# Where large tiles start in SBUF: from 128 bytes past a multiple of 256 to multiples of 256, with two families 160 and 96 bytes past one

## The chip, the cores and the metric

The kernel runs on one core of a Trainium2 chip. The metric is the device time of one launch in microseconds (us). Before the change the median of two runs is 1065.82 us (1065.74 and 1065.90). The host only lays arrays out ahead of the launch.

## What is computed

Two decoder layers and a last RMSNorm, all in float32, for one sequence of 512 positions and a model width of 1024. Cut to what matters:

```
for layer in range(2):
    h = rms_norm(x, norm_g)                              # 512 x 1024
    proj = h @ w_in                                      # 8704 columns, cut into 13 parts
    a = diff_attention(aq, ak, av) * silu(az)            # 4 heads
    c = short_conv(cx, cb, cc, conv_w) * silu(cz)
    r = retention(rq, rk, rv) * silu(rz)                 # 4 heads
    g = sigmoid(gates)                                   # 3 x 1024 columns of proj
    merged = sum(g[i] * ((a, c, r)[i] @ w_branch[i]) for i in range(3))
    x = x + merged @ w_out
out = rms_norm(x, final_norm_g)
```

## The kernel before

Activations lie transposed: channels on the 128 partitions, the 512 positions along the row, so that one tile of 128 x 512 float32 takes 2048 bytes of each partition. Every float32 product is made of three matmuls in `float32r` (`mm3`, lines 190 to 193): an operand is split into a high part, which is rounded, and a low part, which is the rest (`split`, line 186: ScalarE copies the high part, VectorE or GpSimd subtracts), and the three products hi x hi, hi x lo and lo x hi are added up in one PSUM bank. The first operand of `T.matmul` after the output is the stationary one, which LDWEIGHTS loads; the second is the moving one.

Weights come in chunks of 128 x 1024, in the order of `chunk_order`, by one DMA each into `wraw`, and are split into `whi` and `wlo` (4096 bytes of each partition, three buffers each). `proj` (line 422) makes 128 output columns from one chunk: 24 matmuls, whose stationary operands are 128 x 128 slices of `whi` and `wlo` and whose moving operands are the eight pairs of `h` tiles (tag "h", 16 buffers). `merge` (line 621) adds the product of a branch's four pairs of `xb` tiles with a chunk of `w_branch`; its last round leaves the merged rows `m` as eight pairs of tiles with the tag "vm". `out_proj` (line 676) has these `vm` tiles as moving operand and slices of `w_out` as stationary one; in the last layer it works on halves of 256 columns. Before `out_proj` the same 16 buffers hold the values of attention and retention: there `vm` is the stationary operand and the tiles with the tag "st" are the moving one (lines 527 and 611). In `values` (line 367) `xb` is stationary and `whi`/`wlo` are moving.

TensorE's instructions stand in an order that the code gives (`tick` and `at` put the attention and retention steps between the projections); the other engines' order is that of the program, with semaphores where operands ask for them.

All tiles come from three SBUF pools, each a row of tags in the order in which they are first asked for: `small` (the tags in `SMALL`), `sb` (nearly everything) and `odd` (only `wu`, whose rows are 2056 bytes). `t` (line 168) picks the pool by the tag, `tr` (line 172) asks for a `float32r` tile. Because every tag in `sb` takes a multiple of 256 bytes, all tiles of `sb` start at the same place within 256 bytes, and where that is follows from the size of `small`: 128 bytes past a multiple of 256.

Of the kernel before, what the change touches and what calls it, by code (L numbers as in the profile page):

```python
# [10 lines left out]
F32 = mybir.dt.float32  # L11
# [7 lines left out]
P = 128  # L19
# [135 lines left out]
def tile_hybrid_trunk(ctx: ExitStack, tc: tile.TileContext, xT, w, prm, lam, tab, cmat, outT):  # L155
    nc = tc.nc

    def pool(name, bufs=1, **kw):
        return ctx.enter_context(tc.tile_pool(name=name, bufs=bufs, **kw))

    SMALL = ("par", "eps", "lam_e", "ones_p", "ones_d", "nlam0", "nlam1", "gsub0", "gsub1", "rtok", "nm", "sm")
    small, sb, odd = pool("small"), pool("sb"), pool("odd")
    ps = pool("ps", space=PSUM)
# [2 lines left out]
    def t(tag, bufs, shape=(P, S), dt=F32):  # L168
        home = small if tag in SMALL else odd if tag == "wu" else sb
        return home.tile(list(shape), dt, tag=tag, bufs=bufs, name=tag)  # L170

    def tr(tag, bufs, shape=(P, S)):
        return t(tag, bufs, shape, F32R)

    def pj():
        return ps.tile([P, S], F32, tag="pj", bufs=NPJ, name="pj")
# [30 lines left out]
    def split_next():  # L207
        if not raws:
            prefetch()
        if raws:  # L210
            raw = raws.pop(0)
            hi, lo = tr("whi", 3, (P, 1024)), tr("wlo", 3, (P, 1024))
            for c in range(0, 1024, 512):
                c = slice(c, c + 512)
                if pos[0] or parts or c.start:
                    split(hi[:, c], lo[:, c], raw[:, c], G if c.start else V)
                else:
                    V.tensor_copy(hi[:, c], raw[:, c])
                    lo_part(lo[:, c], raw[:, c], hi[:, c])
            parts.append((hi, lo))  # L220
# [53 lines left out]
    nc.sync.dma_start(cm, cmat)  # L274
    ident, negmask, tri = (cm[:, i * P:(i + 1) * P] for i in range(3))
    ones_p = tr("ones_p", 1, (P, P))
    A.copy(ones_p, cm[:, 3 * P:4 * P])
    ones_d = t("ones_d", 1, (P, 1))
# [23 lines left out]

    H = [slice(0, 64), slice(64, 128)]
    klo = [tr("klo", 4) for _ in range(4)]
    for n, lo in enumerate(klo):
        G.memset(lo[H[1 - n % 2]].bitcast(F32), 0.0)
# [44 lines left out]
    for l in range(DEPTH):  # L351
# [59 lines left out]
        h = []  # L411
# [338 lines left out]
```

## Time and profile before

| | |
|---|---|
| median of the runs | 1065.82 us |
| profiled execution, its own time | 1065.34 us |
| its span, first to last instruction | 1063.5 us |
| PE, matmuls | 1053.9 us, 99% of the span, 5010 instructions |
| PEld, weight loads | 881.7 us, 83% |
| DVE (VectorE) | 681.9 us, 64% |
| ACT (ScalarE) | 503.0 us, 47% |
| POOL (GpSimd) | 318.7 us, 30% |
| granted TensorE clock | 0.998 of full speed, the 2.4 GHz level |

Matmuls overlap in the profile: a record runs from the matmul's start to its last result, and the next one starts before that. How fast TensorE goes is therefore read from the distance between two starts, here called the gap; the record is longer than the gap by a constant part in steady running.

### The profile page before, as it was taken

The numbers are of one execution on the slowest core, as the hardware profiler recorded it, in microseconds if no ns is written. First come the engines' busy times: TensorE is split into PE (matmuls) and PEld (weight loads), VectorE is DVE, ScalarE is ACT, GpSimd is POOL, SyncE is SP. The second block draws the span as 40 slices with busy tenths as digits, with TensorE's granted clock in tenths as the row PEclk, the third lists the DMA queues.
The fourth block names the chain that finished last, engine by engine and source line by source line (L and its number), as shares of the span: only waits on it lengthen the run. The fifth ranks groups of instructions, "written<-read, shape, count | busy, mean of one in ns | idle before, by whom it ended". The sixth has DMA issues, their size and how long they took to land.

```text
span 1063.5 us, 13847 instructions
## 1 busy us (share of the span) xinstructions
PE 1053.9 (99%) x5010; PEld 881.7 (83%) x5010; DVE 681.9 (64%) x1168; ACT 503.0 (47%) x943; POOL 318.7 (30%) x253
## 2 busy tenths in 40 slices
PE   9999999999999999999999999999999999999997
PEld 6888888888888888888888888888888888888896
DVE  8687686765677566345528876868556956654444
ACT  6454354543554554334434535445354645543353
POOL 6222232221233333232412212332123233333264
PEclk9999999999999999999999999999999999999999
DMA  6323222232234222444432232223213432133453
GB/s 258 106 93 100 88 71 96 83 119 85 74 119 139 77 85 78 128 129 149 149 99 83 87 109 80 80 84 119 96 60 100 139 100 80 61 107 129 128 190 119
DMA packets 34340, 113.64 MB, mean 107 GB/s; under 512 B 3936, under 2 KB 3936, under 8 KB 34272
## 3 DMA queue, kind: packets, MB, share of 16 engines
q1 hardware_dynamic: 34128, 112.50, 32.4%
q8 instruction: 39, 0.64, 0.3%
q14 instruction: 29, 0.24, 0.1%
q10 hardware_dynamic: 144, 0.26, 0.1%
HBM read 108.55 MB, written 4.19 MB: 106 GB/s over the span
## 4 chain that ended last, share of the span: by engine, by line
PE 93%; DVE 5%; ACT 1%; issue 1%; DMA 0%; SPq 0%; DVEq 0%; ACTq 0%
PE pj L191 28%; PE pj L192 28%; PE pj L193 28%; PE pa L466 3%; PE pa L192 1%; PE pa L193 1%; DVE wa L414 1%; PE pa L191 1%; DVE wlo L184 1%; PE pa L592 1%; DVE h L184 1%; DVE vm L382 1%; ACT h L187 1%; DVE xb L362 0%; PE pa L499 0%
## 5 line engine op out<-in xcount | busy, mean ns | idle before, releaser
L184 POOL TENSOR_TENSOR wlo<-wraw,whi 128x512 fp32r<-128x512 f32 x184 | 251.8, 1371 | 628.0 <-ACT whi L187 582.2
L191 PE MATMUL pj<-h,whi 128*128 128x512 f32 x960 | 379.4, 395 | 0.0
L192 PE MATMUL pj<-h,whi 128*128 128x512 f32 x960 | 374.7, 390 | 0.2
L193 PE MATMUL pj<-h,wlo 128*128 128x512 f32 x960 | 374.7, 390 | 0.0
L187 ACT CAST whi<-wraw 128x512 fp32r<-128x512 f32 x367 | 216.3, 617 | 220.9 <-PE pj L192 141.1
L184 DVE TENSOR_TENSOR wlo<-wraw,whi 128x512 fp32r<-128x512 f32 x184 | 153.1, 833 | 125.5 <-ACT whi L187 124.5
L193 PEld LDWEIGHTS pj<-h,wlo 128*128 128x128 f32 x960 | 180.2, 188 | 38.9 <-DVE wlo L184 0.3
L192 PEld LDWEIGHTS pj<-h,whi 128*128 128x128 f32 x960 | 180.5, 188 | 35.7 <-DVE h L184 1.1
L191 PEld LDWEIGHTS pj<-h,whi 128*128 128x128 f32 x960 | 180.4, 188 | 35.4
L191 PE MATMUL pj<-xb,whi 128*128 128x512 f32 x192 | 75.0, 391 | 0.0
L192 PE MATMUL pj<-xb,whi 128*128 128x512 f32 x192 | 74.9, 390 | 0.0
L193 PE MATMUL pj<-xb,wlo 128*128 128x512 f32 x192 | 74.7, 389 | 0.0
L579 ACT ACTIVATE p<-pa,nm 128x128 f32<-128x128 f32 (+3 forms) x64 | 33.5, 527 | 69.2 <-DVE nm L576 69.0
L503 DVE RECIPROCAL e<-e 128x512 f32<-128x512 f32 x16 | 53.6, 3351 | 18.0 <-ACT e L502 18.0
L187 ACT CAST st<-pa 128x256 fp32r<-128x256 f32 (+2 forms) x80 | 29.8, 373 | 70.5 <-DVE pa L521 40.5
L191 PE MATMUL pj<-vm,whi 128*128 128x256 f32 (+1 forms) x192 | 61.3, 319 | 0.0
L192 PE MATMUL pj<-vm,whi 128*128 128x256 f32 (+1 forms) x192 | 61.1, 318 | 0.0
L193 PE MATMUL pj<-vm,wlo 128*128 128x256 f32 (+1 forms) x192 | 61.1, 318 | 0.0
L636 DVE SCALAR_TENSOR_TENSOR wb<-wa,pj 128x512 f32<-128x512 f32 x32 | 22.0, 687 | 41.5 <-PE pj L193 38.3
L184 DVE TENSOR_TENSOR st<-pa,st 128x256 fp32r<-128x256 f32 (+2 forms) x80 | 33.6, 420 | 17.1 <-ACT st L187 16.5
L193 PEld LDWEIGHTS pj<-xb,wlo 128*128 128x128 f32 x192 | 36.0, 188 | 7.6
L191 PEld LDWEIGHTS pj<-xb,whi 128*128 128x128 f32 x192 | 36.1, 188 | 7.3
(132 smaller groups left out, 1433.6 us busy)
## 6 DMA issues: line engine op xcount, KB each, us to landing
wraw<-w SPq DMA_DIRECT2D x183, 512.0 KB, 3.4
tab<-tab SPq DMA_DIRECT2D x10, 512.0 KB, 3.4
xm<-xT SPq DMA_DIRECT2D x15, 256.0 KB, 3.7
xsave<-xm SPq DMA_DIRECT2D x8, 256.0 KB, 2.0
xm<-xsave SPq DMA_DIRECT2D x8, 256.0 KB, 2.6
outT<-p SPq DMA_DIRECT2D x8, 256.0 KB, 2.1
wraw<-w SPq DMA_DIRECT2D x2, 256.0 KB, 3.4
xm<-xT ACTq DMA_DIRECT2D x1, 256.0 KB, 3.0
```

The lines of the kernel that those rows point to most:

```text
L184: eng.tensor_tensor(lo, x, hi, op=ALU.subtract)
L187: A.copy(hi, x)
L191: T.matmul(out, wh, xh, start=start, stop=False)
L192: T.matmul(out, wh, xl, start=False, stop=False)
L193: T.matmul(out, wl, xh, start=False, stop=stop)
L382: V.scalar_tensor_tensor(lo, banks[tt], rtok[:, tt:tt + 1], hi, op0=ALU.mult, op1=ALU.subtract)
L414: V.scalar_tensor_tensor(hk, x[k], ng[k], rrow, op0=ALU.mult, op1=ALU.mult)
L466: T.matmul(o, ac[i][:, asl], bc[i][:, bsl], start=i == 0, stop=i == 1)
L503: V.reciprocal(r, r)
L579: A.activation(pc[:, :n], sp[:, :n], AF.Exp, bias=nm, scale=0.125, accum_out=sm)
L592: T.transpose(tp[:, j * P:(j + 1) * P], p1[:, j * P:(j + 1) * P], ident)
L636: V.scalar_tensor_tensor(y, g, 1.0, o, op0=ALU.add, op1=ALU.mult)
```

## The change

```
-
     SMALL = ("par", "eps", "lam_e", "ones_p", "ones_d", "nlam0", "nlam1", "gsub0", "gsub1", "rtok", "nm", "sm")
...
+
+    GAP, gaps = {"vm": 40, "h": 48, "st": 40}, {}
+
     def tr(tag, bufs, shape=(P, S)):
+        if tag in GAP and tag not in gaps:
+            gaps[tag] = t("gap_" + tag, 1, (P, GAP[tag]))
         return t(tag, bufs, shape, F32R)
+
+    small.tile([P, 32], F32, tag="fill", bufs=1, name="fill")
```

`fill` puts 128 bytes into `small`, so that the pools behind it start 128 bytes later. When `tr` is first asked for "vm", "h" or "st", a tile of 160, 192 or 160 bytes is put into `sb` ahead of that tag. No instruction reads or writes these tiles. On each of the five engines the changed program has the same instructions with the same waits in the same order; line numbers behind the change are larger by 6. What differs is where tiles start in each partition:

| tiles | bytes past a multiple of 256, before | after |
|---|---|---|
| `wraw`, `xm`, `wa`, `wb`, `xb`, `klo`, `qk`, `whi`, `wlo`, `e1`, `e2` | 128 | 0 |
| `vm` (values; later the merged rows m) | 128 | 160 |
| `h`, `tab`, `ez`, `p0`, `p1` | 128 | 96 |
| `st`, `wc`, `sq`, `wu` | 128 | 0 |
| `ones_p` (in `small`) | 160 | 32 |

## Rows read from the trace of the kernel before

**Rows 1.** The page: the span, engines' busy time (share) and instructions, the chain.
```profile
span 1063.5 us, 13847 instructions
...
PE 1053.9 (99%) x5010; PEld 881.7 (83%) x5010; DVE 681.9 (64%) x1168; ACT 503.0 (47%) x943; POOL 318.7 (30%) x253
...
PE 93%; DVE 5%; ACT 1%; issue 1%; DMA 0%; SPq 0%; DVEq 0%; ACTq 0%
```
**Rows 2.** Groups by form, PE: out<-in, tile, shape, xcount | busy us, mean ns | idle before.
```profile
L191 PE MATMUL pj<-h,whi 128*128 128x512 f32 x960 | 379.4, 395 | 0.0
L192 PE MATMUL pj<-h,whi 128*128 128x512 f32 x960 | 374.7, 390 | 0.2
L193 PE MATMUL pj<-h,wlo 128*128 128x512 f32 x960 | 374.7, 390 | 0.0
...
L191 PE MATMUL pj<-vm,whi 128*128 128x256 f32 x128 | 36.4, 284 | 0.0
...
L191 PE MATMUL pj<-vm,whi 128*128 128x512 f32 x64 | 24.9, 389 | 0.0
...
L193 PE MATMUL pa<-st,vm 128*128 128x256 f32 x40 | 11.3, 283 | 0.0
...
L193 PE MATMUL pa<-st,vm 128*128 128x128 f32 x24 | 6.6, 273 | 0.0
...
L193 PE MATMUL pa<-st,vm 128*128 128x512 f32 x8 | 3.2, 395 | 0.0
...
L193 PE MATMUL pa<-st,vm 128*128 128x384 f32 x8 | 2.7, 336 | 0.0
```
**Rows 3.** Timeline of PE, a steady stretch: start us, record us, engine line op.
```profile
51.93 0.39 PE L191 MATMUL pj<-h,whi 128*128 128x512 f32 x1
52.16 0.39 PE L192 MATMUL pj<-h,whi 128*128 128x512 f32 x1
...
56.69 0.39 PE L191 MATMUL pj<-h,whi 128*128 128x512 f32 x1
```
**Rows 4.** Timeline of PE, the last layer's out_proj.
```profile
1039.72 0.28 PE L193 MATMUL pj<-vm,wlo 128*128 128x256 f32 x1
...
1040.92 0.28 PE L191 MATMUL pj<-vm,whi 128*128 128x256 f32 x1
```
**Rows 5.** Timeline of all engines where a weight load came late.
```profile
22.62 0.39 PE L193 MATMUL pa<-whi,xb 128*128 128x512 f32 x1
22.62 0.19 PEld L191 LDWEIGHTS pj<-whi,xb 128*128 128x128 f32 x1
22.85 0.39 PE L191 MATMUL pj<-whi,xb 128*128 128x512 f32 x1
...
23.38 0.19 PEld L192 LDWEIGHTS pj<-wlo,xb 128*128 128x128 f32 x1 [0.56 <-DVE wlo L184]
23.38 0.50 PE L192 MATMUL pj<-wlo,xb 128*128 128x512 f32 x1
```
**Rows 6.** Timeline of PE around one pair of matmuls with `ones_p`.
```profile
138.18 0.40 PE L193 MATMUL pj<-h,wlo 128*128 128x512 f32 x1
138.42 0.39 PE L499 MATMUL pa<-st,ones_p 128*128 128x512 f32 x1
138.65 0.39 PE L500 MATMUL pa<-st,ones_p 128*128 128x512 f32 x1
...
141.18 0.39 PE L192 MATMUL pj<-h,whi 128*128 128x512 f32 x1
```
**Rows 7.** Timeline of PE behind four short matmuls.
```profile
122.08 0.27 PE L466 MATMUL pa<-klo,qk 128*128 128x128 f32 x1
122.19 0.45 PE L191 MATMUL pj<-h,whi 128*128 128x512 f32 x1
122.47 0.40 PE L192 MATMUL pj<-h,whi 128*128 128x512 f32 x1
```
**Rows 8.** Waits: engine, line, what ended them, us in total, times, longest.
```profile
POOL wlo L184 <- ACT whi L187: 582.2, 154, 8.9
ACT whi L187 <- PE pj L192: 141.1, 85, 5.6
DVE wlo L184 <- ACT whi L187: 124.5, 72, 4.7
```

## The prediction, made before the changed kernel was run

> **What bounds the kernel now.** I began with the page. PE is busy for 99% of the span and the chain of work that ended last runs through PE for 93% of it [rows 1], so only what TensorE does between one matmul's start and the next can move the time by much. The other engines have room: ACT, POOL and part of DVE's work wait for each other and for TensorE for hundreds of microseconds [rows 8].
>
> The groups by form say which matmuls these are. The three lines of `mm3` with `h` as moving operand and 512 columns come 960 times each, 2880 in all; with `vm` moving there are 3 x 64 = 192 of 512 columns and 3 x 128 = 384 of 256 columns; with `vm` stationary there are 3 x (40 + 24 + 8 + 8) = 240 [rows 2].
>
> Then the gap. In the timeline of a steady stretch 21 gaps take 56.69 - 51.93 = 4.76 us, 226.7 ns each [rows 3]. At 2.4 GHz, one column a cycle, 512 columns are 213.3 ns, so 13.3 ns are lost in each. With 256 columns, ten gaps take 1.20 us, 120.0 ns each [rows 4], against 106.7 ns: again 13.3 ns. This loss is what the change could touch. It is in 2880 + 192 + 384 = 3456 matmuls whose two operands move against each other, together 3456 x 13.3 = 46 us, and no more than this can be won in them.
>
> **What the change does, part by part.** It adds no instruction, no wait and no DMA; all engines' rows stand as before. Three things differ.
>
> *Everything 128 bytes further.* `whi`, `wlo`, `xb`, `qk`, `klo`, `st` go from 128 to 0 past a multiple of 256 together. Matmuls between these have both operands moved alike. Nothing in the trace has an operand at 0, so the trace gives no price for this; below, it is one of the ways to the fast rival. I take 0.
>
> *`h` at 96 and `vm` at 160 as moving operands, weights at 0.* Before, both operands of every one of these matmuls start at the same place within 256 bytes; after, they are 96 and 160 bytes apart, and the moving one no longer starts at a multiple of 64. The trace has one matmul whose operands are apart: `ones_p` as stationary operand lies at 160, its moving `st` at 128. Around such a pair the gaps are no longer steady: the load of `ones_p` runs under the matmul before it, whose gap reads 0.24 us and whose record grows from 0.39 to 0.40, and from 138.18 to 141.18 us 13 gaps take 3.00 us, 230.8 ns each, until the steady 0.39 is back [rows 6]. So TensorE does feel where operands start, by 230.8 - 226.7 = 4.1 ns a matmul while it is out of step, and it falls back into step by itself. The same happens behind short matmuls, which disturb the rhythm without any odd address: a record of 0.45 us, a gap of 0.28, then 0.40 [rows 7].
>
> Is the steady loss of 13.3 ns due to the load that runs under the matmul? Where a load came late, by 0.56 us, the matmul at 22.85 us ran without a load under it, and its record is 0.39 us like that of its neighbours [rows 5]. So the 13.3 ns look like the moving operand's own, not a quarrel with the weights. That says the relation of the two addresses has little to win in steady running, and that a new relation shifts the step in which both settle. What it may win is the time out of step: the records of `h` average 395, 390 and 390 ns where 389 is the steady value (the `vm` row with 512 columns), that is 960 x 6 + 960 x 1 + 960 x 1 = 7.7 us over the steady rate [rows 2]. Bounds for this part: -7.7 us if all of it went, +3456 x 4.1 = +14 us if TensorE never got into step. Part of the 7.7 us is the price of short matmuls as such and stays. I take half, -3.8 us.
>
> *`vm` at 160 as stationary operand, `st` at 0.* These 240 matmuls have the shape of the `ones_p` case, 32 bytes off. Between 0 and 240 x 4.1 = +1.0 us; I take +0.5, since two of three matmuls here have 256 or fewer columns and their records of 283 and 273 ns [rows 2] are long against their columns anyhow. The `ones_p` pair itself stays 32 bytes off, 16 pairs at 13 x 4.1 = 0.05 us, 0.9 us in all, unchanged.
>
> On VectorE, ScalarE and GpSimd the same operations read and write at new places. Their cover is their waiting: 582 us of POOL's and 124 us of DVE's idle time is for ACT's split, and 141 us of ACT's is for TensorE [rows 8]. If that cover failed in one place, the next weight load would be late, as in rows 5, at about half a microsecond each time. I take 0.
>
> Sum, against the profiled execution: 1065.3 - 3.8 + 0.5 = 1062.0 us. Its own time is 1065.34 us, span 1063.5 plus 1.8 around it; the median of the runs is 0.5 us above it, which I leave aside.
>
> **A rule against the change.** Rows 5 show a matmul that is no shorter without a load under it, and rows 6 a load that lengthens the matmul above it. The Trainium skill, page "TensorE: Matmul & The Clock Gate", section "Step-by-step: what each phase is for", says that TensorE reads the moving operand and the weights through two independent ports, so that loading weights takes nothing from the running matmul. By that rule where the two start against each other can't matter, and the sum would be the time before, 1065.3 us; rows 5 agree with it (0.39 us either way), rows 6 do not.
>
> **Rivals.**
>
> *Nothing moves.* The steady gap is the moving operand's own and the same at any of these places, and TensorE settles as often as before. For it: rows 5, and that the same 226.7 ns and 389 ns stand for `h`, `xb` and `vm`. Against it: rows 6. Time: 1065.3 us, or 1065.8 by the median. Chance 0.16.
>
> *Faster by over one step: the loss in the steady gap goes down.* The change sets the moving operands 96 and 160 bytes off the weights, on either side of half of 256. If the 13.3 ns (32 cycles) come from both reads starting at the same place within 256 bytes in the same hundredth of a microsecond (22.62 and 22.62 in rows 5), setting them apart takes half or all of it away. Half: 3456 x 6.7 = 23 us, 1042 us. All: 46 us, 1019 us. It passes 2% (21.3 us) when the gap of 512 columns falls to about 220.5 ns. For it: the loss is there in each matmul, and all matmuls of the trace but those with `ones_p` have both operands at the same place, so the trace has never shown another relation in steady running. Against it: rows 5, and that the only other relation made gaps longer. Chance 0.31, of which 0.28 passes 2%. The same page's section "Back-to-back issue gap" gives N/2.4 + 2.5 ns as the spacing, 215.8 ns for 512 columns; by it there would be an estimated 3456 x 10.9 = 38 us to win, 1028 us, while the trace shows 226.7.
>
> *Slower: TensorE no longer gets into step.* All 3456 matmuls get operands that are an odd multiple of 32 bytes apart, as those with `ones_p` are, and the disturbance that rows 6 show for a single pair becomes the rule. At the mean of that stretch, 4.1 ns, it is +14 us: 1079 us. At 6 ns it is +21 us, 1086 us, which is where it passes 2%; at the loss of one more 13.3 ns it would be +46 us, 1111 us. For it: the sign in rows 6. Against it: the stretch in rows 6 ends by itself within 13 matmuls. Chance 0.21, of which 0.17 passes 2%.
>
> **How the numbers follow.** The forecast, within 2% and slightly faster, has 0.32. Below 1027 us lies the part of the fast rival in which nearly all of the loss goes, about 0.08; above 1086 us the worse part of the slow one, about 0.12. So the range is 1027 to 1086 us; the likeliest case's own range is 1057.6 (all of the 7.7 us) to 1068. Over 2% (about what a measurement of this kernel can tell from no change) faster: 0.28. Within 2%: 0.32 + 0.16 + 0.03 + 0.04 = 0.55. Slower: 0.17.
>
> **What would show it.** Right: the steady gap with `h` in the timeline is still 226 to 227 ns, records 389 ns, and the means of 395, 390 and 390 ns fall by up to 6, 1 and 1. The fast rival: steady gaps at or below 220 ns, records of `h` at 383 ns or less, `vm` with 256 columns below 120. The slow one: means of `h` at 393 ns and above, gaps that change from matmul to matmul through whole projections. The part for `vm` as stationary operand is wrong if the 256-column row of 283 ns moves by more than 4. The forecast as a whole is wrong if the 13.3 ns depend on where the moving operand itself starts, which no row of before can show.

## The result and the profile after

The changed kernel takes 1084.01 us (1083.72 and 1084.30) against 1065.82 before: a ratio of 1.0171, with a 95% interval of 1.0154 to 1.0188. It is slower by 18.2 us. The forecast said 1062, slightly faster; the time lies in its range, on the side of the slow rival.

First the page of the changed kernel: span, busy times, the chain.

```profile
span 1082.5 us, 13847 instructions
...
PE 1071.8 (99%) x5010; PEld 881.2 (81%) x5010; DVE 681.2 (63%) x1168; ACT 502.9 (46%) x943; POOL 319.3 (29%) x253
...
PE 97%; DVE 1%; ACT 0%; DMA 0%; issue 0%; SPq 0%; DVEq 0%; ACTq 0%
```

The span has grown by 19.0 us and PE's busy time by 17.9, against [rows 1]. No other engine's busy time has moved by more than 0.7 us. So it is the matmuls themselves that take longer; the 1.1 us by which PE's idle time has grown is for the most part waiting for low parts of weights, in the last row below (0.3 us before, 1.6 now). Which matmuls, the groups by form of PE say (lines 197 to 199 are 191 to 193 of before):

```profile
L197 PE MATMUL pj<-h,whi 128*128 128x512 f32 x960 | 383.4, 399 | 0.0
L199 PE MATMUL pj<-h,wlo 128*128 128x512 f32 x960 | 380.2, 396 | 0.0
L198 PE MATMUL pj<-h,whi 128*128 128x512 f32 x960 | 379.6, 395 | 0.0
...
L198 PE MATMUL pj<-xb,whi 128*128 128x512 f32 x192 | 75.5, 393 | 0.0
...
L197 PE MATMUL pj<-vm,whi 128*128 128x256 f32 x128 | 36.1, 282 | 0.0
...
L197 PE MATMUL pj<-vm,whi 128*128 128x512 f32 x64 | 25.4, 396 | 0.0
...
L198 PE MATMUL pj<-wlo,xb 128*128 128x512 f32 x64 | 25.2, 393 | 1.6 <-DVE wlo L190 1.6
```

Two rows of before that [rows 2] does not show:

```profile
L191 PE MATMUL pj<-xb,whi 128*128 128x512 f32 x192 | 75.0, 391 | 0.0
L192 PE MATMUL pj<-xb,whi 128*128 128x512 f32 x192 | 74.9, 390 | 0.0
```

With `h` the mean records rise from 395, 390 and 390 ns [rows 2] to 399, 395 and 396. With `vm` and 512 columns they rise from 389 to 396. With `vm` and 256 columns they fall, from 284 to 282. And the matmuls of `xb`, whose two operands have both moved alike, rise too (390 to 393 on the line shown).

The timeline of PE at the same 21 matmuls as in [rows 3] shows what a steady stretch looks like now:

```profile
52.51 0.40 PE L197 MATMUL pj<-h,whi 128*128 128x512 f32 x1
52.75 0.40 PE L198 MATMUL pj<-h,whi 128*128 128x512 f32 x1
...
57.42 0.39 PE L197 MATMUL pj<-h,whi 128*128 128x512 f32 x1
```

21 gaps take 4.91 us, 233.8 ns each instead of 226.7, and records of 0.39 and 0.40 us alternate to the end of the stretch. TensorE never gets into the step of before.

Taking all starts of both traces in order and subtracting gap from gap, the 19.0 us are: 15.4 in the 2880 matmuls with `h` (5.4 ns each), 1.5 in the 192 of 512 columns with `vm` (7.6 ns each), 1.5 in the 576 with `xb` moving, 0.5 in the 384 with `xb` stationary, minus 0.5 in the 384 of 256 columns, and 0.6 in small groups. The 0.5 with `xb` stationary is not the change's: the same sum gives 0.5 there in the run below with all tiles at 160, in which no two of these operands are apart.

### The profile page after: what moved, and what is told of

It is laid out like the page before. It is cut to its first block, busy times and chain, and to the rows that moved or that the text cites. A ratio compares the mean times of both kernels' runs of the same rounds, so it can differ in the third digit from the quotient of the medians.

```text
span 1082.5 us, 13847 instructions
## 1 busy us (share of the span) xinstructions
PE 1071.8 (99%) x5010; PEld 881.2 (81%) x5010; DVE 681.2 (63%) x1168; ACT 502.9 (46%) x943; POOL 319.3 (29%) x253
## 4 chain that ended last, share of the span: by engine, by line
PE 97%; DVE 1%; ACT 0%; DMA 0%; issue 0%; SPq 0%; DVEq 0%; ACTq 0%
PE pj L197 29%; PE pj L198 29%; PE pj L199 29%; PE pa L472 3%; PE pa L199 2%; PE pa L198 2%; PE pa L197 2%; PE pa L598 1%; DMA xm<-xT 0%; DVE xb L368 0%; PE pa L506 0%; PE pa L505 0%; DVE p L714 0%; DVE e L333 0%; PE pa L341 0%
## 5 line engine op out<-in xcount | busy, mean ns | idle before, releaser
L197 PE MATMUL pj<-h,whi 128*128 128x512 f32 x960 | 383.4, 399 | 0.0
L199 PE MATMUL pj<-h,wlo 128*128 128x512 f32 x960 | 380.2, 396 | 0.0
L198 PE MATMUL pj<-h,whi 128*128 128x512 f32 x960 | 379.6, 395 | 0.0
```

Of the source, the lines that this page charges most:

```text
L197: T.matmul(out, wh, xh, start=start, stop=False)
L198: T.matmul(out, wh, xl, start=False, stop=False)
L199: T.matmul(out, wl, xh, start=False, stop=stop)
```

## Experiments

Three theories were set against each other. R: the distance between the starts of a matmul's two operands, taken within some number of bytes, sets whether TensorE gets into step. M: it is the place of the moving operand alone. F: it is the move of everything by 128 bytes.

### One part of the change at a time, and all tiles moved together

The fill alone, without gaps:

```
-    GAP, gaps = {"vm": 40, "h": 48, "st": 40}, {}
+    GAP, gaps = {}, {}
```

> Only the 128 bytes of fill, no gaps: all large tiles at 0 past a multiple of 256. Theory R (the distance between the two operands of a matmul, within 256 bytes, sets whether TensorE gets into step): distance 0 as before, so 1065.8 us and a steady gap of 226.7 ns. Theory M (it is where the moving operand itself starts: a multiple of 64 is good, 32 past one is bad): the same 1065.8 us. Theory F (starting at 0 past 256 instead of 128 costs or wins something): the time differs from 1065.8, up to all of the +18.2 us.

Measured: 1065.60 us, ratio 1.000 (0.9991 to 1.0009). F falls: for all tiles together, 0 and 128 past a multiple of 256 are the same.

`h` alone at 96, `vm` at 0:

```
+    GAP, gaps = {"h": 24, "st": 40}, {}
```

> Fill, and h alone moved to 96 past a multiple of 256; vm at 0 (tab, ez and the attention weights also at 96, as in the change). Theories R and M: the 2880 matmuls with h rise by 5.4 ns as in the changed kernel, +15.5 us, 1081 us. Theory F: 1084 as with the fill alone. If the cost were in vm instead: 1066 us.

Measured: 1082.45 us, ratio 1.0159 (1.0142 to 1.0176). The groups by form show the rise with `h` and nothing with `vm`:

```profile
L197 PE MATMUL pj<-h,whi 128*128 128x512 f32 x960 | 383.5, 399 | 0.0
...
L197 PE MATMUL pj<-vm,whi 128*128 128x512 f32 x64 | 24.9, 389 | 0.0
```

`vm` alone at 160, `h` at 0:

```
+    GAP, gaps = {"vm": 40, "h": 24}, {}
```

> Fill, and vm alone moved to 160 past a multiple of 256; h at 0. Theories R and M: 192 matmuls of 512 columns rise by 7.5 ns (+1.4 us), the 384 of 256 columns fall by 1 ns (-0.4 us), 240 with vm as stationary operand between 0 and +1 us: 1066.5 to 1068 us, and the matmuls with h keep 226.7 ns. Theory F: 1084.

Measured: 1066.71 us, ratio 1.0009 (0.9999 to 1.0018). The interval just takes in no change; the rows say where the microsecond is:

```profile
L197 PE MATMUL pj<-h,whi 128*128 128x512 f32 x960 | 379.3, 395 | 0.0
...
L197 PE MATMUL pj<-vm,whi 128*128 128x256 f32 x128 | 36.1, 282 | 0.0
...
L197 PE MATMUL pj<-vm,whi 128*128 128x512 f32 x64 | 25.4, 396 | 0.0
```

The parts add up: +16.8 (`h`) and +1.0 (`vm`), 17.8 us of the 18.2.

All large tiles at 160, which is no multiple of 64, but all operands at distance 0:

```
-    small.tile([P, 32], F32, tag="fill", bufs=1, name="fill")
+    small.tile([P, 8], F32, tag="fill", bufs=1, name="fill")
-    GAP, gaps = {"vm": 40, "h": 48, "st": 40}, {}
+    GAP, gaps = {}, {}
```

> Fill of 32 bytes in place of 128 and no gaps: all large tiles start at 160 past a multiple of 256, that is 32 past a multiple of 64, and the two operands of each matmul are 0 apart. Theory R: 1065.8 us, steady gap 226.7 ns. Theory M: all 4152 matmuls of 512 columns are disturbed by 5 to 7.5 ns, 1087 to 1097 us.

Measured: 1065.58 us, ratio 0.9999 (0.9990 to 1.0008), with `h` back at the records of before:

```profile
L197 PE MATMUL pj<-h,whi 128*128 128x512 f32 x960 | 379.4, 395 | 0.0
```

M falls. As far as was tried (0, 128 and 160), where all operands start together does not matter; how far the two are apart does.

### The distance measured by itself

A kernel that runs TensorE alone: streams of 48 matmuls, each stream with another place of its operands. It leaves the reference's computation out and ran once.

```
+    def stream(name, so, mo, n=512, count=48):
+        o = ps.tile([P, S], F32, tag="o", bufs=4, name=name)
+        for i in range(count):
+            s0 = so // 4 + 128 * (i % 7)
+            m0 = mo // 4
+            T.matmul(o[:, 0:n], sta[:, s0:s0 + P], mov[i % 2][:, m0:m0 + n], start=i == 0, stop=i == count - 1)
...
```

> Not the reference's computation: TensorE alone runs streams of 48 matmuls of 512 columns (and, half_, 256 columns) in float32r, with no other engine at work. In mov_ streams the moving operand starts 0 to 224 bytes past a multiple of 256 and the stationary at 0; in sta_ streams the stationary is moved and the moving one at 0; in both_ streams both are moved alike; three more have the moving operand at 8, 16 and 48. Theory R64 (the distance counts within 64 bytes): a settled gap of 226.7 ns (record 389 ns) at 0, 64, 128 and 192, and 231 to 238 ns at 32, 96, 160 and 224, in mov_ and sta_ alike; 226.7 in all of both_. Theory R256 (it counts within 256): 64, 128 and 192 also differ from 226.7, each in its own way. Theory W (some distance takes the 13.3 ns loss away): at one of them the gap falls to 214 to 220 ns. If the work of other engines is what disturbs matmuls whose operands are apart: 226.7 everywhere here.

The timeline of PE, merged by stream: start us, us, line, operation, stream. The distance from one start to the next, divided by 48, is the gap.

```profile
18.79 11.04 PE L186 MATMUL mov_zero<-mov,sta 128*128 128x512 f32 x48
29.67 11.37 PE L186 MATMUL mov_thirtytwo<-mov,sta 128*128 128x512 f32 x48
40.88 11.16 PE L186 MATMUL mov_sixtyfour<-mov,sta 128*128 128x512 f32 x48
51.88 11.37 PE L186 MATMUL mov_ninetysix<-mov,sta 128*128 128x512 f32 x48
63.09 11.36 PE L186 MATMUL mov_onetwentyeight<-mov,sta 128*128 128x512 f32 x48
74.28 11.40 PE L186 MATMUL mov_onesixty<-mov,sta 128*128 128x512 f32 x48
85.53 11.35 PE L186 MATMUL mov_oneninetytwo<-mov,sta 128*128 128x512 f32 x48
96.72 11.35 PE L186 MATMUL mov_twotwentyfour<-mov,sta 128*128 128x512 f32 x48
107.91 11.06 PE L186 MATMUL sta_zero<-mov,sta 128*128 128x512 f32 x48
...
174.79 11.16 PE L186 MATMUL sta_oneninetytwo<-mov,sta 128*128 128x512 f32 x48
185.78 11.36 PE L186 MATMUL sta_twotwentyfour<-mov,sta 128*128 128x512 f32 x48
...
229.70 11.08 PE L186 MATMUL both_ninetysix<-mov,sta 128*128 128x512 f32 x48
240.61 11.08 PE L186 MATMUL both_onetwentyeight<-mov,sta 128*128 128x512 f32 x48
...
284.27 5.91 PE L186 MATMUL half_zero<-mov,sta 128*128 128x256 f32 x48
290.01 5.82 PE L186 MATMUL half_thirtytwo<-mov,sta 128*128 128x256 f32 x48
295.67 5.82 PE L186 MATMUL half_sixtyfour<-mov,sta 128*128 128x256 f32 x48
301.33 5.91 PE L186 MATMUL half_ninetysix<-mov,sta 128*128 128x256 f32 x48
307.07 5.86 PE L186 MATMUL half_onetwentyeight<-mov,sta 128*128 128x256 f32 x48
...
318.47 5.82 PE L186 MATMUL half_oneninetytwo<-mov,sta 128*128 128x256 f32 x48
324.12 5.84 PE L186 MATMUL half_twotwentyfour<-mov,sta 128*128 128x256 f32 x48
```

| moving minus stationary, within 256 bytes | gap, 512 columns, ns |
|---|---|
| 0 | 226.7 (10.88 / 48) |
| 32 | 233.5 (11.21 / 48) |
| 64 | 229.2 (11.00 / 48) |
| 96 | 233.5 |
| 128 | 233.1 |
| 160 | 234.4 |
| 192 | 233.1 |
| 224 | 233.1 |

Starts are read to 0.01 us, so these gaps are good to some 0.2 ns. Moving the stationary operand instead gives the same by the difference, within 0.3 ns and at 128 within 1: `sta_oneninetytwo` is a distance of 64 and takes 229.0 ns. Moving both by 96 takes 227.3 ns, the odd half nanosecond being the start of the stream (the last 30 gaps take 226.9). So the theory is R with 256 bytes: of the eight distances 0 is the only one at which each gap is 226 or 227 ns. At 96 the gaps run in a cycle of three, 238, 230 and 232 ns, from the eighth on: TensorE settles there too, but at a longer mean. The two moving tiles of a stream lie 0 and 256 bytes past a multiple of 512, and the gap of 226.7 holds across both, so 256 is a whole turn. That another distance would take the loss of 13.3 ns away (W) falls at 512 columns. With 256 columns 0 is no longer the best: 119.6 ns at 0 and as much at 96, against 117.9 at 32 and 64 and 117.7 at 192.

No other engine worked here, so the disturbance needs no other engine's work.

### Back in the kernel: h at 64 and at 192

```
-    GAP, gaps = {"vm": 40, "h": 48, "st": 40}, {}
+    GAP, gaps = {"h": 16, "st": 48}, {}
```

for 64 and, for 192,

```
-    GAP, gaps = {"vm": 40, "h": 48, "st": 40}, {}
+    GAP, gaps = {"h": 48, "st": 16}, {}
```

> All large tiles at 0 past a multiple of 256, h alone at 64. Theory R256 by the streams measured alone (settled gap 228.9 ns with the moving operand 64 past the stationary one, against 226.7 at 0): 2880 x 2.2 = +6.3 us, 1072 us. Theory R64 (only the distance within 64 bytes counts): 1065.7 us. If the cost in the kernel came with every other place alike: 1082 us as with h at 96.

Measured: 1074.61 us, ratio 1.0093 (1.0077 to 1.0108), +9.2 us on the runs of before beside it. R64 falls, and the order of the table holds, but the rise is 2.9 us more than the 6.3 expected.

> The same with h at 192. Theory R256: settled gap 233.3 ns at 192, 2880 x 6.7 = +19 us at most, and as h at 96 gave 16.8 us of the 19.2 that its 233.3 ns stand for, some 1082 to 1085 us. Theory R64: 1065.7 us. If 64 on either side were alike: 1072 us.

Measured: 1081.34 us, ratio 1.0149 (1.0135 to 1.0163), +15.9 us, as much as `h` at 96 within a microsecond, and 0.7 below what was expected. 64 on either side are not alike, as in the table.

Where the 2.9 us are, the rows of `h` at 64 say:

```profile
L197 PE MATMUL pj<-h,whi 128*128 128x512 f32 x960 | 382.8, 399 | 0.0
...
L197 PE MATMUL pj<-xb,whi 128*128 128x512 f32 x192 | 75.8, 395 | 0.0
```

The matmuls with `h` cost 6.9 us by their gaps, 2.4 ns each, close to the 2.2 to 2.5 of the stream. The rest stands in others: +1.5 us in those with `xb` moving, whose own distance is 0 (395 ns here against 391 before), +0.3 in the values, which is within what that group moved by with nothing apart, and 0.3 in small groups. Those with `xb` moving run between matmuls with `h` and have to get into step anew each time.

### Neighbours, other widths and bfloat16

> Not the reference's computation: TensorE streams again, of 128 and 384 columns in float32r, of 512 columns in bfloat16 at eight distances, and twelve groups of six float32r matmuls of 512 columns that take turns between distance 0 and 96. Theory R256: with 128 columns the weight load is the bound (110 to 113 ns) and the distance counts little; 384 columns at 0 differ from those apart. In bfloat16, if the loss comes with the 4-byte rate of reading, 216 ns or so at every distance; if with the address alone, a spread of some ns again. The groups of six: if a matmul with its operands together pays for its neighbours' distance, those at 0 have a gap over 229 ns instead of 226.7.

Streams again, without the reference's computation; the timeline merged by stream, of the second such kernel, which ran once too:

```profile
39.96 8.54 PE L186 MATMUL long_zero<-mov,sta 128*128 128x384 f32 x48
48.34 8.48 PE L186 MATMUL long_sixtyfour<-mov,sta 128*128 128x384 f32 x48
56.65 8.64 PE L186 MATMUL long_ninetysix<-mov,sta 128*128 128x384 f32 x48
65.13 8.49 PE L186 MATMUL long_onesixty<-mov,sta 128*128 128x384 f32 x48
...
83.83 10.52 PE L203 MATMUL bf_thirtytwo<-movb,stab 128*128 128x512 bf16 x47
94.19 10.52 PE L203 MATMUL bf_sixtyfour<-movb,stab 128*128 128x512 bf16 x47
...
159.13 1.55 PE L186 MATMUL gapc<-mov,sta 128*128 128x512 f32 x6
160.52 1.57 PE L186 MATMUL gapd<-mov,sta 128*128 128x512 f32 x6
161.93 1.55 PE L186 MATMUL gape<-mov,sta 128*128 128x512 f32 x6
163.32 1.56 PE L186 MATMUL gapf<-mov,sta 128*128 128x512 f32 x6
```

`gapc` and `gape` have distance 0, `gapd` and `gapf` 96. A group of six at distance 0 takes 1.39 us, 231.7 ns a matmul; one at 96 takes 1.40 or 1.41. So a matmul at distance 0 pays for its neighbours, as in the kernel. With 384 columns the gaps are 174.6, 173.1, 176.7 and 173.5 ns at 0, 64, 96 and 160; the last 30 at 0 take 173.3, so there 96 alone stands out. With 128 columns they are 110.6 to 111.7 at the four distances tried. In bfloat16 a stream takes 10.36 us; each sent 48 matmuls, one of whose records is missing, so 215.8 ns. Seven of the eight distances take that within 0.01 us; at 224 the next stream started 0.19 us sooner, and its gaps are the same 215 to 217 ns. Neither the loss of 13.3 ns nor the distance shows there.

### A version that is faster than both

Two places of the kernel before are not at their best distance by the streams: the pairs with `ones_p` at 224, and the 256-column matmuls of the last `out_proj` at 0.

```
-    SMALL = ("par", "eps", "lam_e", "ones_p", "ones_d", ...
+    SMALL = ("par", "eps", "lam_e", "ones_d", ...
+    HALVES = [(DEPTH - 1, ("O", c)) for c in range(8)]
...
-            hi, lo = tr("whi", 3, (P, 1024)), tr("wlo", 3, (P, 1024))
+            off = 16 if order[pos[0] + len(parts)] in HALVES else 0
+            hi, lo = (tr(tag, 3, (P, 1088))[:, off:off + 1024] for tag in ("whi", "wlo"))
```

> The kernel before, with ones_p moved among the large tiles (distance 0 instead of 224 for its 32 matmuls) and, in the last layer's out_proj alone, the slices of w_out 64 bytes further, so that its 384 matmuls of 256 columns have the moving operand at 192 from the stationary one. Theory R256: the ones_p pairs cost no stretch out of step, 16 x 0.053 = -0.85 us; the 256-column gap falls from 120.0 to 117.8 ns as in the streams alone, 384 x 2.2 = -0.85 us; together 1064.0 us, with 227 ns around ones_p in the trace. If 256 columns gain only without other engines at work: 1064.9. Theory R64: the 256-column gap stays at 120.0.

Measured: 1063.43 us against 1065.44 of the runs of before beside it, ratio 0.9980 (0.9972 to 0.9989). A small gain, with no change outside its interval, and it stands where the streams put it. Groups by form, then the timeline around the pair of [rows 6]:

```profile
L191 PE MATMUL pj<-vm,whi 128*128 128x256 f32 x128 | 36.0, 281 | 0.0
...
L501 PE MATMUL pa<-st,ones_p 128*128 128x512 f32 x16 | 6.2, 389 | 0.0
```

```profile
138.20 0.39 PE L193 MATMUL pj<-h,wlo 128*128 128x512 f32 x1
138.43 0.39 PE L501 MATMUL pa<-st,ones_p 128*128 128x512 f32 x1
...
141.15 0.39 PE L192 MATMUL pj<-h,whi 128*128 128x512 f32 x1
```

The 13 gaps that took 3.00 us in [rows 6] take 2.95, 226.9 ns each. By the gaps of the whole trace the 256-column matmuls give 1.1 us and the stretches behind `ones_p` 0.8.

## Why the prediction was wrong

**The bound and the matmuls counted** were right: PE alone moved, and 16.4 of the 19.0 us came from the 3456 matmuls with operands apart. Of the rest 1.5 came from their neighbours with `xb` moving.

**"Everything 128 bytes further" at 0** was right: the fill alone gives a ratio of 1.000.

**The step that failed** is "it falls back into step by itself". The stretch in [rows 6] does end within 13 matmuls, but those that follow the `ones_p` pair have their operands at distance 0. From the two matmuls that were apart one can't read what a stream of such matmuls does; I took the recovery of the aligned ones behind them for a property of TensorE. The stream at one constant distance shows that it does not settle at 226.7 (233.5 ns at 96). So the term "I take half, -3.8 us" of the time out of step had the wrong sign; in its place stands +15.4 us for `h` and +1.5 for `vm` with 512 columns. By the stream's 6.8 ns the 2880 matmuls with `h` would cost an estimated 19.6 us; that they cost 15.4 fits the prediction's reading that some time was lost out of step before (395, 390 and 390 ns against 389), which is argued here and not tested. [Rows 6] also had the sign right, and they were the only rows shown with another distance; the forecast went against the one row that bore on it.

**The reading of the late load** ([rows 5]: a matmul without a load under it is no shorter, so the 13.3 ns are not a quarrel with the weights) fits what was measured: no distance takes them away at 512 columns. From it I went on to say that the relation of the two addresses had little to win, which holds, and let that stand for little to lose, which does not follow. At distance 0 the load costs the matmul above it nothing visible; at other distances the matmuls of the streams take 2 to 8 ns more.

**The slow rival** was the right mechanism. Its 4.1 ns, the mean of the recovery in [rows 6], was 5.4 for `h` and 7.6 for `vm` with 512 columns, and its 14 us came out as 18.2. It did not have the neighbours (1.5 us with `xb` moving) or the gain with 256 columns (-0.5 us). That the operands are an odd multiple of 32 bytes apart is not what counts in it: 128 and 192 cost as much as 96 in the streams, and 64 costs 2.5 ns.

**`vm` as stationary operand**: forecast +0.5 us; by the gaps these 240 matmuls moved by 0.1 us, and by 0.2 with `vm` alone at 160. The matmuls around them pay too: with `vm` alone at 160, all groups but those with `vm` moving, the values and the ten bfloat16 matmuls at the start rise by some 0.4 us against the fill alone, so the forecast was right in size. Of the 240, four in five and not two in three have 256 or fewer columns [rows 2].

**The fast rival** is ruled out for 512 columns by the streams: 226.7 is the least of the eight distances. Its other half, that setting the operands apart wins something, is true of the widths tried with 256 columns alone, by 1 to 2 ns, and not at 96. Its price through the spacing of the Trainium skill's page "TensorE: Matmul & The Clock Gate", section "Back-to-back issue gap" (215.8 ns for 512 columns), describes the bfloat16 streams here (215.8), not float32r (226.7).

**The rule of independent ports** (the same page of the Trainium skill, section "Step-by-step: what each phase is for") would have left the time as it was. Where the operands start has moved it by 1.7% here, so for float32r at 512 columns the measurement decides against taking it as a rule on time. Whether the two reads meet in a port, in the memory or elsewhere, these runs do not show; that a weight load and the moving operand of the matmul above it disturb each other is argued from the distance being between just these two, and a stream without loads was not tried. Two traces point to the next weights, which load under a matmul, rather than to its own. In [rows 6] the first long gap, 234 or 235 ns at each of the 16 pairs, is that of the matmul before the pair, whose own operands are at distance 0. With `vm` alone at 160 each of the 36 matmuls of 512 columns that stand right before one with `vm` as weights takes 236 or 237 ns, with its own operands at distance 0, where the fill alone gives 226 or 227; one of them, in that run:

```profile
169.46 0.40 PE L199 MATMUL pj<-h,wlo 128*128 128x512 f32 x1
169.69 0.28 PE L197 MATMUL pa<-st,vm 128*128 128x256 f32 x1
```

What happens between the two reads is not shown by this. The few matmuls of `h` with a late load, and so with none under them, do not settle it either: with `h` at 96 such a matmul reads 0.39 us (the one at 57.42 above), with `h` at 192 0.40, where its neighbours there read 0.39.

What stays open: where the two reads meet and how, why a whole turn is 256 bytes, and why 64 is better than the other six.

## What to carry to other kernels

Where matmuls in float32r stream 512 columns and TensorE is the bound, let the stationary and the moving operand start at the same place within 256 bytes; the place itself was free in all that was tried. In this kernel a pool of their own for the small tiles does it, because every other tag is a multiple of 256 bytes. At 256 columns distance 0 was 2 ns a matmul worse than 32, 64 or 192, and in bfloat16 the distance made no difference, so such a rule is to be measured for the width and type at hand. A single odd instruction among regular ones shows the sign of an effect, but how it dies away belongs to its neighbours; the price of a stream of them has to come from a stream.

## What the runs showed of the hardware that I had not expected

- A matmul of 512 columns in float32r takes 226.7 ns from start to start at its best, 13.3 more than its columns at 2.4 GHz (granted clock 1.00 in that stream); in bfloat16 215.8.
- Distances of 8, 16 and 48 bytes between the operands were tried in the first streams too: 233.3, 231.7 and 230.0 ns by their starts. The effect is not one of multiples of 32 or 64.
- Being out of step is contagious: matmuls at distance 0 in groups of six between others take 231.7 ns instead of 226.7.
